# Modulation vectors of a two-layer decoder trunk: other phases, another pace, and VectorE for all

## Chip, core and metric

One core of a Trainium2 chip runs the whole kernel. The metric is the device time of one execution in microseconds. TensorE (PE in the profile, PEld for its weight loads), VectorE (DVE), ScalarE (ACT), GpSimd (POOL) and SyncE (SP, which issues nearly all DMAs) work at the same time and wait for one another by semaphores.

## The reference

Two layers over 256 tokens of width 1024. Each is a feed-forward block, a mixer of four parallel branches and another feed-forward block, and each of the three is modulated by three vectors (shift, scale, gate) that come from a conditioning vector `c`. There are nine such vectors of 1024 values per layer, each a product of `silu(c)` with a 1024x1024 slice of `ada_w`.

```python
D_MODEL, SEQ, DEPTH, D_FF, N_ADA = 1024, 256, 2, 2816, 9
def modulate(x, shift, scale): return x * (1.0 + scale) + shift
def swiglu(u, w1, w3, w2):     return (jax.nn.silu(u @ w1) * (u @ w3)) @ w2
# one layer, m = nine modulation vectors of c; s, b, g = shift, scale, gate of a phase
#   x = x + 0.5*(1+g1) * swiglu(modulate(rmsnorm(x), s1, b1))          first feed-forward
#   x = x + (1+g2) * W_out(sum_b sigmoid(G_b) * P_b(branch_b(u)))      mixer, u = modulate(rmsnorm(x), s2, b2)
#   x = x + 0.5*(1+g3) * swiglu(modulate(rmsnorm(x), s3, b3))          second feed-forward
# branches: RG-LRU (convolution + scan), latent attention, indexer-sparse attention, diagonal S5
```

## The kernel before

**Precision and tiling.** All weights lie in DRAM as float32. Each weight tile of 512 KB is loaded by a DMA of SyncE into a `raw` buffer (five of them), ScalarE rounds it into `hi` (`S.copy`, the CAST of L237), VectorE forms the rest `lo = raw - hi` (L103, L238), and TensorE does three matmuls for each product: hi·hi, hi·lo, lo·hi (`mm3`, `mm3w`, L243 to L251). The activations `uh`, `ul` are split in the same way (L371 for `uh`). So each weight tile costs one DMA, one ScalarE cast and one VectorE subtraction, and the split is emitted at a high priority.

**Phases.** Per layer: `ffn` (phase 0), `mixer` (phase 1), `ffn` (phase 2). The text calls them ffn1, mixer and ffn2. In the mixer an order written out by hand (`ORDER`, L66) calls the stages one after another: `za`, `zc`, `zb` are pieces of the input projection, `xr` the RG branch (convolution `r_conv`, matmuls L991 into `ps_acc_rg_states`), `us` and `S1` the S5 branch's input and states (L863, `ps_acc_s_states`; VectorE's `p_s_states`), `S2`, `GL`, `ix`, `m`, `da` the rest of the branches and the two attentions, `gnh` a half of gate n, `pnh` a half of branch projection n with its merge, `t0`, `t1` the merged halves, then `w_out` (`ps_acc_mixer`).

**Modulation vectors.** `ada(l, j)` (L265) is a generator that computes vector j of layer l in nine steps. Eight steps each load 512 KB of `ada_w` into a `raw` buffer (L274) and add its product with a column of `c`: on VectorE into `acc` (one `tensor_scalar`, L280, and seven `scalar_tensor_tensor`, recorded at L106), or, where `ADA_PE` names the vector, on TensorE into a PSUM bank (L277). A vector on VectorE is closed on TensorE by a sum over partitions with a matrix of ones (L287, eight matmuls in the profile). The ninth step's work adds the bias (`mrow`, L103/L294), and writes gates (j mod 3 = 2) to DRAM (L298, L300) or transposes shifts and scales on TensorE (L305, two matmuls) into a column (L307). Sixteen vectors are computed in this way; vectors 0 and 1 of layer 0 at the program's beginning are done otherwise.

**Pace.** `ADA` (L43) lists which vectors belong to which phase, as numbers j, where 9 and above are vectors of the next layer. `RATE` (L44) is the pace: each weight tile constructed (class `W`, L219) calls `tick()` (L210), which adds the phase's rate to a counter and runs one step of the generator for every whole number:

```python
    def tick():
        bg["n"] += bg["rate"]
        while bg["n"] >= 1.0:
            bg["n"] -= 1.0
            next(bg["gen"], None)
```

The stage `a` of `ORDER` runs whatever is left of the generator. Up to where `a` stands in the new order, a mixer constructs 70 weight tiles. Vectors 6 and 7 of a layer (shift and scale of its ffn2) are needed when the mixer's tail forms the next `uh` (`inputs_of`, L1489), vectors 3 and 4 when ffn1's tail does, vectors 2, 5 and 8 as gates in the tails of the three phases.

## Time and profile before

| | us |
|---|---|
| median of 3 runs | 1500.77 |
| lowest, highest run | 1494.9, 1513.13 |
| profiled execution | 1495.38 |
| span of its trace, first to last instruction | 1493.6 |
| TensorE busy | 1413.4 (95%) |
| VectorE busy | 1175.4 (79%) |
| ScalarE busy | 770.0 (52%) |
| mean granted clock of TensorE | 0.990 of full speed |

The phases of the span begin with the first u-matmul of each: the mixer of layer 0 at 245 us, its ffn2 at 580, ffn1 of layer 1 at 777, the mixer of layer 1 at 985, its ffn2 at 1301. Busy times of several engines lie over one another. A granted clock of 1.00 is 2.4 GHz, 0.50 is 1.2 GHz. A timeline entry with "x4" stands for four instructions of one kind in a row. The name behind "<-" in brackets is what ended the engine's idle time.

### The profile page before, as it was taken

Reading aid. Unit: us, or ns where it says so; the run is one execution under the profiler, and the core shown is the slowest. Engines: PE = TensorE matmul, PEld = TensorE weight load, DVE = VectorE, ACT = ScalarE, POOL = GpSimd, SP = SyncE. Lnnn points to the kernel's source line nnn. Section 1 sums busy time; section 2 is a strip of 40 time slices with the busy share of each in tenths; the row PEclk is TensorE's granted clock in tenths of the full one; section 3 lists DMA queues with packets and bytes.
Section 4 is the critical chain, followed back from the end, with each engine's and each line's share of the span. In section 5 each row is a group of like instructions: output and inputs, shape, how many; then the busy total and the mean of one; then the engine's idle time right before and its main releaser. Section 6 shows DMA issues by size and latency. Waiting matters only on the chain.

```text
span 1493.6 us, 26644 instructions
## 1 busy us (share of the span) xinstructions
PE 1413.4 (95%) x10310; PEld 1262.7 (85%) x10310; DVE 1175.4 (79%) x2027; ACT 770.0 (52%) x1223; POOL 64.0 (4%) x75
## 2 busy tenths in 40 slices
PE   8899999899998998999989998999999999999998
PEld 4588987789888897999968887879988879799997
DVE  4598988789897577988787888777998956866655
ACT  4444456654475645544453445568445655544442
POOL 0000000001011000000010000000100100000000
PEclk9999999999999999999999999999999999999999
DMA  9788888786435365899977878755653535567762
GB/s 287 236 288 291 280 260 258 228 222 174 114 117 138 99 187 181 286 328 317 320 252 250 271 254 276 246 135 143 174 146 95 140 94 164 162 214 227 235 203 99
DMA packets 242087, 313.24 MB, mean 210 GB/s; under 512 B 28088, under 2 KB 169256, under 8 KB 241960
## 3 DMA queue, kind: packets, MB, share of 16 engines
q1 hardware_dynamic: 241960, 311.53, 67.0%
q8 instruction: 81, 1.33, 0.4%
q14 instruction: 46, 0.38, 0.1%
HBM read 310.41 MB, written 1.07 MB: 209 GB/s over the span
## 4 chain that ended last, share of the span: by engine, by line
PE 55%; DVE 21%; DMA 11%; issue 6%; ACT 5%; POOL 1%; SPq 1%; POOLq 0%; DVEq 0%; ACTq 0%
DVE lo_genexpr L103 7%; DMA raw_ada<-in_ada_w_dram 5%; PE ps_up_up_half L249 5%; PE ps_up_up_half L250 5%; PE ps_up_up_half L251 5%; DMA raw_init<-in_ffn_w_dram 4%; PE ps_acc_down_proj L246 3%; PE ps_acc_down_proj L245 3%; PE ps_acc_down_proj L244 3%; PE ps_up_gate L250 3%; ACT hi_genexpr L237 3%; PE ps_up_gate L249 3%; PE ps_up_gate L251 3%; DVE acc_ada L106 2%; PE ps_up_merge L250 2%
## 5 line engine op out<-in xcount | busy, mean ns | idle before, releaser
L237 ACT CAST hi_genexpr<-raw_init 128x1024 fp32r<-128x1024 f32 (+2 forms) x430 | 441.1, 1028 | 497.2 <-PE ps_up_up_half L250 127.4
L103 DVE TENSOR_TENSOR lo_genexpr<-raw_init,hi_genexpr 128x1024 fp32r<-128x1024 f32 (+2 forms) x430 | 511.5, 1193 | 152.5 <-ACT hi_genexpr L237 150.1
L249 PE MATMUL ps_up_up_half<-uh_new_u,hi_genexpr 128*128 128x256 f32 x1216 | 339.2, 279 | 4.2 <-DVE p_silu_cols L106 1.6
L250 PE MATMUL ps_up_up_half<-ul_new_u,hi_genexpr 128*128 128x256 f32 x1216 | 337.4, 278 | 0.0
L251 PE MATMUL ps_up_up_half<-uh_new_u,lo_genexpr 128*128 128x256 f32 x1216 | 337.2, 278 | 0.1
L249 PEld LDWEIGHTS ps_up_up_half<-uh_new_u,hi_genexpr 128*128 128x128 f32 x1216 | 228.8, 188 | 9.8 <-issue 7.5
L250 PEld LDWEIGHTS ps_up_up_half<-ul_new_u,hi_genexpr 128*128 128x128 f32 x1216 | 228.7, 188 | 1.4
L251 PEld LDWEIGHTS ps_up_up_half<-uh_new_u,lo_genexpr 128*128 128x128 f32 x1216 | 228.2, 188 | 0.7 <-DVE lo_genexpr L103 0.7
L106 DVE SCALAR_TENSOR_TENSOR acc_ada<-raw_ada,c_col_tile_trunk,acc_ada 128x1024 f32<-128x1024 f32 x105 | 134.4, 1280 | 28.6 <-DMA raw_ada<-in_ada_w_dram 28.2
L250 PE MATMUL ps_up_gate<-ul_new_u,hi_genexpr 128*128 128x256 f32 x512 | 144.8, 283 | 0.0
L249 PE MATMUL ps_up_gate<-uh_new_u,hi_genexpr 128*128 128x256 f32 x512 | 144.6, 282 | 0.0
L251 PE MATMUL ps_up_gate<-uh_new_u,lo_genexpr 128*128 128x256 f32 x512 | 143.6, 280 | 0.0
L246 PE MATMUL ps_acc_down_proj<-hi_genexpr,yT_mul_cols 128*128 128x512 f32 x288 | 114.6, 398 | 0.0
L244 PE MATMUL ps_acc_down_proj<-hi_genexpr,yT_mul_cols 128*128 128x512 f32 x288 | 114.5, 397 | 0.0
L245 PE MATMUL ps_acc_down_proj<-lo_genexpr,yT_mul_cols 128*128 128x512 f32 x288 | 114.3, 397 | 0.1
L249 PEld LDWEIGHTS ps_up_gate<-uh_new_u,hi_genexpr 128*128 128x128 f32 x512 | 96.4, 188 | 3.0 <-issue 2.2
L251 PEld LDWEIGHTS ps_up_gate<-uh_new_u,lo_genexpr 128*128 128x128 f32 x512 | 96.7, 189 | 0.9 <-issue 0.8
L250 PEld LDWEIGHTS ps_up_gate<-ul_new_u,hi_genexpr 128*128 128x128 f32 x512 | 96.4, 188 | 1.1 <-issue 1.0
L244 PEld LDWEIGHTS ps_acc_down_proj<-hi_genexpr,yT_mul_cols 128*128 128x128 f32 x288 | 54.1, 188 | 13.1 <-issue 1.6
L245 PEld LDWEIGHTS ps_acc_down_proj<-lo_genexpr,yT_mul_cols 128*128 128x128 f32 x288 | 54.2, 188 | 12.6 <-DVE lo_genexpr L103 0.6
L246 PEld LDWEIGHTS ps_acc_down_proj<-hi_genexpr,yT_mul_cols 128*128 128x128 f32 x288 | 54.1, 188 | 12.3
L244 PE MATMUL ps_up_tok_gemm<-hi_genexpr,uh_new_u 128*128 128x424 f32 (+2 forms) x88 | 33.8, 385 | 2.7 <-ACT gt_gate L112 2.7
(474 smaller groups left out, 2698.1 us busy)
## 6 DMA issues: line engine op xcount, KB each, us to landing
raw_init<-in_ffn_w_dram SPq DMA_DIRECT2D x240, 512.0 KB
raw_ada<-in_ada_w_dram SPq DMA_DIRECT2D x128, 512.0 KB
raw_init<-in_w_in_dram SPq DMA_DIRECT2D x96, 512.0 KB
raw_init<-in_w_branch_dram SPq DMA_DIRECT2D x24, 512.0 KB
raw_init<-in_ffn_w_dram SPq DMA_DIRECT2D x36, 256.0 KB
raw_init<-in_w_out_dram SPq DMA_DIRECT2D x16, 512.0 KB
s5p_load<-in_ada_w_dram SPq DMA_DIRECT2D x16, 256.0 KB
s5p_load<-in_ada_w_dram SPq DMA_DIRECT2D x8, 512.0 KB
```

The lines of the kernel that those rows point to most:

```text
L103: eng.tensor_tensor(o, x, y, op)
L106: V.scalar_tensor_tensor(o, x, s, y, op0, op1)
L237: S.copy(self.hi, self.raw)
L244: T.matmul(o, xh, wh, start=first, stop=False)
L245: T.matmul(o, xh, wl, start=False, stop=False)
L246: T.matmul(o, xl, wh, start=False, stop=last)
L249: T.matmul(o, wh, xh, start=first, stop=False)
L250: T.matmul(o, wh, xl, start=False, stop=False)
L251: T.matmul(o, wl, xh, start=False, stop=last)
```

## The change

Four things. `ADA` gives two vectors (6 and 7) to the mixer of layer 1, which had none, and takes one each from ffn2 of layer 0 (five to four) and from ffn1 of layer 1 (four to three); sixteen vectors are computed as before. `RATE` lowers the pace of both mixers to 0.27 steps a weight tile (from 1.03 and 1.0), and of those two feed-forwards to 0.65 and 0.52. The TensorE variant of the product is gone: vector 7 of layer 0, the one that used it, goes to VectorE. And the stage `a` moves in `ORDER` from behind `gr S1` to behind `g21`, near the mixer's end.

```diff
-ADA = (((2, 3, 4, 5), (6, 7), (8, 9, 10, 11, 12)), ((4, 5, 6, 7), (), (8,)))
-RATE = ((0.67, 1.03, 0.81), (0.68, 1.0, 0.2))
+ADA = (((2, 3, 4, 5), (6, 7), (8, 9, 10, 11)), ((3, 4, 5), (6, 7), (8,)))
+RATE = ((0.67, 0.27, 0.65), (0.52, 0.27, 0.2))
-ADA_PE = ((7, 10, 9, 11), ())
-ORDER = """za xr xr us xr S1 xr g01 S1 gr S1 a zc S1 g00 S1 ix S2 g30 p01 S2 g20 S2 ix ix p00 ix m S2 S2 m m g31 zb m GL da p30 ix m m p31 da g10 da m m g11 p20 p10 g21 p11 p21 t0 t1"""
+ORDER = """za xr xr us xr S1 xr g01 S1 gr S1 zc S1 g00 S1 ix S2 g30 p01 S2 g20 S2 ix ix p00 ix m S2 S2 m m g31 zb m GL da p30 ix m m p31 da g10 da m m g11 p20 p10 g21 a p11 p21 t0 t1"""
     def ada(l, j):
-        on_pe = j in ADA_PE[l % 2]
-        if on_pe:
-            p = bank("ms")
-        else:
-            acc = new("acc", (128, 1024))
+        acc = new("acc", (128, 1024))
         for k in range(KD):
...
-            if on_pe:
-                for q in range(4):
-                    T.matmul(p[32 * q:32 * q + 32, 0:256], bc(c_col[:, k:k + 1], (128, 32)), raw[:, 256 * q:256 * q + 256],
-                             start=(k == 0), stop=(k == KD - 1), tile_position=(0, 32 * q))
-            elif k == 0:
+            if k == 0:
                 V.tensor_scalar(acc, raw, c_col[:, k:k + 1], None, OP.mult)
...
-        if not on_pe:
-            p = bank("ms")
-            for q in range(4):
-                T.matmul(p[32 * q:32 * q + 32, 0:256], ones, acc[:, 256 * q:256 * q + 256], start=True, stop=True,
-                         tile_position=(0, 32 * q))
+        p = bank("ms")
+        for q in range(4):
+            T.matmul(p[32 * q:32 * q + 32, 0:256], ones, acc[:, 256 * q:256 * q + 256], start=True, stop=True,
+                     tile_position=(0, 32 * q))
```

Lines of the new kernel stand about ten lower: L106 becomes L105, L103 becomes L102, L287 becomes L277, L305 becomes L295.

VectorE in the mixer of layer 0, at the convolution of the RG branch (`r_conv` rows), before: two steps of vector 6 (`acc_ada`) stand in twelve rows. Each row is line, operation, output<-inputs, shape.

```order
L103 TENSOR_TENSOR mll_mla_in_2757<-ps_tp_ev_2840,mlh_mla_in_2756 128x3x128
L106 SCALAR_TENSOR_TENSOR r_conv_2885<-r_conv_2882,vt_params_699,r_conv_2885 128x256
L975 MEMSET r_conv_2924 128x3
L106 SCALAR_TENSOR_TENSOR acc_ada_2853<-raw_ada_3050,c_col_tile_trunk_86,acc_ada_2853 128x1024
L103 TENSOR_TENSOR lo_genexpr_3117<-raw_init_3114,hi_genexpr_3116 128x1024
L106 SCALAR_TENSOR_TENSOR r_conv_2885<-r_conv_2882,vt_params_699,r_conv_2885 128x256
L106 SCALAR_TENSOR_TENSOR r_conv_2927<-r_conv_2924,vt_params_699,r_conv_2927 128x256
L975 MEMSET r_conv_2966 128x3
L106 SCALAR_TENSOR_TENSOR acc_ada_2853<-raw_ada_3085,c_col_tile_trunk_86,acc_ada_2853 128x1024
L103 TENSOR_TENSOR lo_genexpr_3152<-raw_init_3149,hi_genexpr_3151 128x1024
L106 SCALAR_TENSOR_TENSOR r_conv_2927<-r_conv_2924,vt_params_699,r_conv_2927 128x256
L106 SCALAR_TENSOR_TENSOR r_conv_2969<-r_conv_2966,vt_params_699,r_conv_2969 128x256
```

The same place now:

```order
L105 SCALAR_TENSOR_TENSOR r_conv_2881<-r_conv_2878,vt_params_699,r_conv_2881 128x256
L965 MEMSET r_conv_2917 128x3
L105 SCALAR_TENSOR_TENSOR r_conv_2881<-r_conv_2878,vt_params_699,r_conv_2881 128x256
L105 SCALAR_TENSOR_TENSOR acc_ada_2970<-raw_ada_3137,c_col_tile_trunk_86,acc_ada_2970 128x1024
L102 TENSOR_TENSOR lo_genexpr_3070<-raw_init_3067,hi_genexpr_3069 128x1024
L105 SCALAR_TENSOR_TENSOR r_conv_2881<-r_conv_2878,vt_params_699,r_conv_2881 128x256
L105 SCALAR_TENSOR_TENSOR r_conv_2920<-r_conv_2917,vt_params_699,r_conv_2920 128x256
L965 MEMSET r_conv_2956 128x3
L105 SCALAR_TENSOR_TENSOR r_conv_2920<-r_conv_2917,vt_params_699,r_conv_2920 128x256
L102 TENSOR_TENSOR lo_genexpr_3102<-raw_init_3099,hi_genexpr_3101 128x1024
L105 SCALAR_TENSOR_TENSOR r_conv_2920<-r_conv_2917,vt_params_699,r_conv_2920 128x256
L105 SCALAR_TENSOR_TENSOR r_conv_2959<-r_conv_2956,vt_params_699,r_conv_2959 128x256
```

One step is left among these rows. The numbers count the buffers in the order in which they are taken, so this step, on `raw_ada_3137`, stands ahead of the subtraction `lo` 3070 of a weight tile whose load was issued before. Over the whole convolution, five steps stood among the rows and one does now.

TensorE in the mixer of layer 0, in a gate (`ps_up_gate`), before: one of the eight places at which vector 7 is multiplied.

```order
L250 MATMUL ps_up_gate_3237<-ul_new_u_2577,hi_genexpr_3287 128x256
L251 MATMUL ps_up_gate_3237<-uh_new_u_2576,lo_genexpr_3288 128x256
L249 MATMUL ps_up_gate_3237<-uh_new_u_2576,hi_genexpr_3287 128x256
L250 MATMUL ps_up_gate_3237<-ul_new_u_2577,hi_genexpr_3287 128x256
L251 MATMUL ps_up_gate_3237<-uh_new_u_2576,lo_genexpr_3288 128x256
L277 MATMUL ps_ms_ada_3291<-raw_ada_3330,c_col_tile_trunk_86 32x256 x4
```

Now there is no such place; what a vector has on TensorE is its closing sum and, eight rows later, its two transposes, here those of vector 6 in `g20`:

```order
L248 MATMUL ps_up_gate_4145<-uh_new_u_2576,hi_genexpr_4148 128x256
L249 MATMUL ps_up_gate_4145<-ul_new_u_2577,hi_genexpr_4148 128x256
L250 MATMUL ps_up_gate_4145<-uh_new_u_2576,lo_genexpr_4149 128x256
L277 MATMUL ps_ms_ada_4182<-acc_ada_2970,ones_tile_trunk_98 32x256 x4
L248 MATMUL ps_up_gate_4145<-uh_new_u_2576,hi_genexpr_4178 128x256
L249 MATMUL ps_up_gate_4145<-ul_new_u_2577,hi_genexpr_4178 128x256
L250 MATMUL ps_up_gate_4145<-uh_new_u_2576,lo_genexpr_4179 128x256
L248 MATMUL ps_up_gate_4145<-uh_new_u_2576,hi_genexpr_4178 128x256
L249 MATMUL ps_up_gate_4145<-ul_new_u_2577,hi_genexpr_4178 128x256
L250 MATMUL ps_up_gate_4145<-uh_new_u_2576,lo_genexpr_4179 128x256
L248 MATMUL ps_up_gate_4145<-uh_new_u_2576,hi_genexpr_4178 128x256
L295 MATMUL ps_tp_ada_4194<-cst_tile_trunk_75,mrow_ada_4192 128x128 x2
```

The eight groups of `L277 x4` are gone; the closing sum and the transposes of a vector stand within one gate, with matmuls of that gate between them.

VectorE in the mixer of layer 1, at the S5 states (`p_s_states`), before:

```order
L103 TENSOR_TENSOR lo_genexpr_12091<-raw_init_12088,hi_genexpr_12090 128x1024
L103 TENSOR_TENSOR b_s_states_11586<-p_s_states_11763,p_s_states_11764 128x4x63
L103 TENSOR_TENSOR b_s_states_11586<-p_s_states_11764,p_s_states_11763 128x4x63
L103 TENSOR_TENSOR p_s_states_11869<-p_s_states_11869,p_s_states_11870 128x256 x2
L103 TENSOR_TENSOR s_rope_12030<-dc_dsa_in_11777,cosT_tile_trunk_101 128x64
L874 SCALAR_TENSOR_TENSOR p_s_states_11870<-s5p_s_prep_9965,p_s_states_11869 128x256
L103 TENSOR_TENSOR lo_genexpr_12121<-raw_init_12118,hi_genexpr_12120 128x1024
L874 SCALAR_TENSOR_TENSOR p_s_states_11870<-s5p_s_prep_9965,p_s_states_11869 128x256
L103 TENSOR_TENSOR s_rope_12031<-dc_dsa_in_11777,sinT_tile_trunk_100 128x64
L103 TENSOR_TENSOR p_s_states_11869<-p_s_states_11870,s5p_s_prep_10118 128x512
L103 TENSOR_TENSOR s_rope_12032<-dc_dsa_in_11777,cosT_tile_trunk_101 128x64
```

The same place now:

```order
L102 TENSOR_TENSOR lo_genexpr_12007<-raw_init_12004,hi_genexpr_12006 128x1024
L102 TENSOR_TENSOR p_s_states_11674<-p_s_states_11674,s5p_s_prep_10041 128x512
L102 TENSOR_TENSOR p_s_states_11782<-p_s_states_11782,p_s_states_11783 128x256
L102 TENSOR_TENSOR b_s_states_11493<-p_s_states_11673,p_s_states_11674 128x4x63
L102 TENSOR_TENSOR b_s_states_11493<-p_s_states_11674,p_s_states_11673 128x4x63
L102 TENSOR_TENSOR lo_genexpr_12037<-raw_init_12034,hi_genexpr_12036 128x1024
L102 TENSOR_TENSOR p_s_states_11782<-p_s_states_11782,p_s_states_11783 128x256
L105 SCALAR_TENSOR_TENSOR acc_ada_11100<-raw_ada_11866,c_col_tile_trunk_86,acc_ada_11100 128x1024
L102 TENSOR_TENSOR lo_genexpr_12072<-raw_init_12069,hi_genexpr_12071 128x1024
L864 SCALAR_TENSOR_TENSOR p_s_states_11783<-s5p_s_prep_9874,p_s_states_11782 128x256 x2
L869 MEMSET b_s_states_11790 128x8
L102 TENSOR_TENSOR s_rope_11946<-dc_dsa_in_11687,cosT_tile_trunk_101 128x64
```

A step of vector 6 of layer 1 (`acc_ada_11100`) has come between two weight tiles' subtractions.

## Rows read from the trace of the kernel before

**Rows 1.** The page's first part: busy time, share of the span, instructions.

```profile
PE 1413.4 (95%) x10310; PEld 1262.7 (85%) x10310; DVE 1175.4 (79%) x2027; ACT 770.0 (52%) x1223; POOL 64.0 (4%) x75
```

**Rows 2.** Table by stretch: start:end, us, busy us (count) PE PEld DVE ACT POOL, clock, DMA share, GB/s.

```profile
245.00:580.00 335.00, 313.16 (x2435) 285.23 (x2436) 270.32 (x544) 187.49 (x356) 22.65 (x22) 0.98 0.57 162
580.00:777.00 197.00, 190.79 (x1340) 171.76 (x1339) 167.76 (x249) 94.27 (x122) 1.55 (x2) 1.00 0.87 297
...
985.00:1301.00 316.00, 299.41 (x2358) 276.47 (x2358) 259.47 (x527) 186.77 (x356) 20.77 (x20) 1.00 0.50 142
```

**Rows 3.** Timeline of PE where the phases begin: start, us, instruction, [idle before <-releaser].

```profile
245.09 0.72 PE L244 MATMUL ps_up_tok_gemm<-dq_genexpr,uh_new_u 128*128 128x416 f32 x1 [2.17 <-ACT uh_new_u L371]
...
579.68 0.50 PE L244 MATMUL ps_up_up_proj<-s5p_genexpr,uh_new_u 128*128 128x512 f32 x1 [2.78 <-ACT uh_new_u L371]
...
776.80 0.79 PE L244 MATMUL ps_up_up_proj<-s5p_genexpr,uh_new_u 128*128 128x512 f32 x1 [2.77 <-ACT uh_new_u L371]
...
985.28 0.46 PE L244 MATMUL ps_up_tok_gemm<-dq_genexpr,uh_new_u 128*128 128x416 f32 x1 [1.00 <-ACT uh_new_u L371]
...
986.86 0.45 PE L246 MATMUL ps_up_tok_gemm<-dq_genexpr,ul_new_u 128*128 128x416 f32 x1 [0.93 <-DVE ul_new_u L103]
...
1301.07 0.50 PE L244 MATMUL ps_up_up_proj<-s5p_genexpr,uh_new_u 128*128 128x512 f32 x1 [1.01 <-ACT uh_new_u L371]
```

**Rows 4.** Tile ps_acc_s_states, window of either mixer: ns min/median/max, first to last start.

```profile
L863 PE MATMUL ps_acc_s_states<-b_s_states,s5p_s_prep x64: 217/275/275, 309.7 to 351.9; 128*128 128x64 f32 x64
...
L863 PE MATMUL ps_acc_s_states<-b_s_states,s5p_s_prep x64: 217/275/323, 1036.0 to 1076.0; 128*128 128x64 f32 x64
```

**Rows 5.** Table by stretch, short windows in the two mixers, columns as in group 2.

```profile
245.00:265.00 20.00, 19.91 (x117) 19.13 (x117) 17.00 (x29) 12.77 (x34) 3.04 (x3) 0.85 0.78 223
265.00:285.00 20.00, 15.42 (x98) 14.29 (x97) 15.75 (x27) 10.55 (x21) 0.06 (x1) 0.83 0.83 240
...
1060.00:1076.00 16.00, 16.00 (x135) 15.97 (x134) 16.00 (x33) 8.06 (x15) 0.00 (x0) 1.00 0.68 187
```

**Rows 6.** Timeline of PE in the mixer of layer 0, columns as in group 3.

```profile
271.90 0.89 PE L991 MATMUL ps_acc_rg_states<-r_conv,rgw_tile_trunk 128*128 128x256 f32 x3 [1.18 <-issue]
...
275.87 1.62 PE L991 MATMUL ps_acc_rg_states<-r_conv,rgw_tile_trunk 128*128 128x256 f32 x3 [2.87 <-DVE r_conv L106]
...
299.79 0.44 PE L305 MATMUL ps_tp_ada<-cst_tile_trunk,mrow_ada 128*128 128x128 f32 x2 [2.63 <-DVE mrow_ada L103]
300.15 0.64 PE L277 MATMUL ps_ms_ada<-raw_ada,c_col_tile_trunk 128*32 128x256 f32 x8
```

**Rows 7.** Timeline of DVE in the mixer of layer 0, columns as in group 3.

```profile
272.12 1.28 DVE L106 SCALAR_TENSOR_TENSOR acc_ada<-raw_ada,c_col_tile_trunk,acc_ada 128x1024 f32<-128x1024 f32 x1
...
274.45 1.67 DVE L106 SCALAR_TENSOR_TENSOR r_conv<-r_conv,vt_params,r_conv 128x256 f32<-128x256 f32 x4
```

**Rows 8.** Tile raw_ada, whole span: operations, and who waited for the tile (us, times).

```profile
L106 DVE SCALAR_TENSOR_TENSOR acc_ada<-raw_ada,c_col_tile_trunk,acc_ada x105: 1262/1279/1289, 77.1 to 1412.1; 128x1024 f32<-128x1024 f32 x105
...
L277 PE MATMUL ps_ms_ada<-raw_ada,c_col_tile_trunk x64: 379/390/403, 300.2 to 327.7; 128*32 128x256 f32 x64
L280 DVE TENSOR_SCALAR acc_ada<-raw_ada,c_col_tile_trunk x15: 739/746/2939, 71.5 to 1311.2; 128x1024 f32<-128x1024 f32 x15
...
  DVE acc_ada L106: 28.2, 33
```

**Rows 9.** Tiles acc_ada and mrow_ada, whole span, columns as in group 8.

```profile
L287 PE MATMUL ps_ms_ada<-acc_ada,ones_tile_trunk x120: 379/391/403, 112.5 to 1438.7; 128*32 128x256 f32 x120
...
  PE ps_tp_ada L305: 5.7, 4
```

**Rows 10.** Tile ps_acc_down_proj, the second feed-forwards of layers 0 and 1, columns as in group 4.

```profile
L246 PE MATMUL ps_acc_down_proj<-hi_genexpr,yT_mul_cols x76: 390/399/402, 635.0 to 773.6; 128*128 128x512 f32 x76
...
L246 PE MATMUL ps_acc_down_proj<-hi_genexpr,yT_mul_cols x76: 390/399/403, 1356.2 to 1488.7; 128*128 128x512 f32 x76
```

**Rows 11.** Waits of DVE in 245 to 580: who <- releaser: us, times, longest.

```profile
DVE acc_ada L280 <- DMA raw_ada<-in_ada_w_dram: 0.6, 1, 0.6
```

## The prediction

> **What bounds the kernel now.** The first look is at the busy times of the whole span: TensorE has work in 1413.4 of 1493.6 us [rows 1], so at most 80 us of waiting is there to win, plus what a lower clock costs. The second is the table by phase [rows 2]: the mixer of layer 0 leaves TensorE idle for 335.0 − 313.2 = 21.8 us at a mean granted clock of 0.98, the second feed-forward of layer 0 moves 297 GB/s at a DMA share of 0.87, and the mixer of layer 1, which has no modulation vector, leaves VectorE idle for 316.0 − 259.5 = 56.5 us, at clock 1.00.
>
> The third look compares the two mixers, which do the same work apart from two vectors. Each begins with its first u-matmul, at 245.09 and 985.28 [rows 3]. The last state matmul of the S5 branch starts at 351.9 and 1076.0 [rows 4], so 106.8 and 90.7 us later: layer 0 is 16.1 us behind after a third of its mixer. Over the whole phase, to the next feed-forward's first matmul (579.68 and 1301.07), it is 334.6 against 315.8, or 18.8 longer. Of these, 1.8 is the longer wait at the end (2.78 against 1.01, [rows 3]), so 17.0 belong to the mixer and nearly all of them arise in the stretch where both vectors stand.
>
> What happens there, in two 20 us windows and the timelines: the clock granted is 0.85 and 0.83 of full speed [rows 5], that is (0.15 + 0.17) × 20 = 6.4 us of full-speed work lost; TensorE waits 1.18, 2.87 and 2.63 us (together 6.7) [rows 6], the second for a row of the RG convolution on VectorE, the third for a vector's result row. VectorE at that moment alternates `r_conv` rows with `acc_ada` steps of 1.28 us; [rows 7] shows one of each, right before the 2.87 us wait ends. Vector 7, on TensorE, has eight groups of eight matmuls of 0.64 us a group [rows 6], 64 in all [rows 8], 5.1 us. That makes 18.2 against the 17.0 of the comparison, which is close since layer 1 has small waits of its own.
>
> **The change part by part.** The sum starts from the profiled execution, 1495.4 us (span 1493.6); the median of the runs shown, 1500.8, lies 5.4 above it.
>
> 1. *The vectors of mixer 0 leave the first 80 us.* The rate of 1.03 becomes 0.27 steps a weight tile, so vector 6, with nine steps, ends near the 9 / 0.27 = 34th of 70 tiles and vector 7 near the 67th, and one step instead of five stands among the convolution rows. Vector 7 costs TensorE no 64 matmuls. So the 17.0 us should come back, but part of the clock loss in the first window follows the phase change: the granted clock was low right behind the 2.17 us wait at 245.09. That window lost 0.15 × 20 = 3.0 us; I leave half, 1.5, in place. Gain: −15.5. At the two ends it is −17.0, or nothing if the waits only move to other rows.
>
> 2. *What two spread vectors cost a mixer; call it c.* No row of before shows a vector strung over a mixer. Each has on VectorE 0.746 + 7 × 1.279 = 9.70 us [rows 8], 19.4 for two, in a phase with 56.5 us of VectorE idle in layer 1. TensorE must still issue the closing sum (eight matmuls, as 120 for 15 vectors [rows 9]; by the group of eight in rows 6 0.64 us) and two transposes, 0.44 [rows 6]: 2.2 us for two vectors. It waits for the result row 5.7 us in all [rows 9] in ten transposing vectors (16 less the six gates, by the code), 0.57 each, 1.1 for two. And the steps find VectorE full in the S5 stretch (16.00 of 16 us [rows 5]), where a step of 1.28 pushes a `lo` that TensorE needs: one such per vector, 2.6. So c = 2.2 + 1.1 + 2.6 = 5.9. Bounds: 2.2, since TensorE's own share can't hide while it is the bound (that also excludes a gain in layer 1, where nothing is removed); and 19.4 + 2.2 = 21.6 if every step lies on the path. I take 5.9, nearer to the low end, because 56.5 us of idle is three times the load.
>  Mixer 0: +5.9. Mixer 1, which had none: +5.9.
>
> 3. *One vector fewer in ffn2 of layer 0 (5 to 4) and in ffn1 of layer 1 (4 to 3).* The price per vector is read from ffn2: with five vectors 579.68 to 773.6 = 193.9 us, with one 1301.07 to 1488.7 = 187.6 [rows 3, 10]; 6.3 for four, 1.6 each. Bounds: 0.64, the closing sum alone, and 10.3, all its VectorE time and that sum. I take 1.6, the one direct comparison, for both: −3.2. The eight loads of 512 KB each move along with the vector, from phases with a DMA share of 0.87 to one with 0.50 [rows 2].
>
> 4. *The change from ffn2 to layer 1.* TensorE waits 2.77 us there, for ScalarE's `uh`, where the crossing into mixer 1 has 1.00 + 0.93 and that into the last phase begins with 1.01 [rows 3]. In the new order no `hi` cast stands between ScalarE's last tail piece and the `uh` casts. I take 2.77 − 1.93, −0.8 (ends: 0 and −2.8).
>
> 5. *The drain `a` at the end of the mixer* is at no cost: by then at most the last of 18 steps is left, and what it hides behind is the gate matmuls of `g21`. If steps remained, each would cost 1.28.
>
> Sum: −15.5 + 5.9 + 5.9 − 3.2 − 0.8 = −7.7, so 1495.4 − 7.7 = **1487.7 us**.
>
> One rule speaks against step 2. In rows 8 the `acc_ada` steps had VectorE waiting for their load 33 times, 28.2 us in all, or 0.27 us for each of 105 steps. The Trainium skill, in "TensorE: Matmul & The Clock Gate", section "Architectural detail: the array is 16× 32×32, not 1× 128×128", says that only TensorE's queue may pull weight loads ahead, and that VectorE and ScalarE work strictly first in, first out; so a step whose load is late holds every `lo` behind it. By the row's 0.27 us a step that is 16 × 0.27 = 4.3 us a mixer at most, and the sum would be 1487.7 + 2 × 4.3 = 1496.3; where it also starves TensorE, it is the third rival.
>
> **The rivals.** A change of 2%, 30 us, is about what a measurement of this kernel can tell from none.
>
> *Nothing is gained.* The 15.5 come back but the vectors cost as much again: c of (15.5 + 3.2 + 0.8) / 2 = 9.8, half of the VectorE time. For it: VectorE is full for tens of us in the S5 stretch, where the new order now has steps. Against: 56.5 us of idle. About 1495.
>
> *Larger gain.* Spread steps all fit into idle time, c = 2.2, and the whole 17.0 comes back: 1495.4 − 17.0 + 4.4 − 4.0 = 1478.8, with the 4.0 of the parts 3 and 4. For it: feed-forward hides a vector at 1.6, which is below my 2.9. Against: the transposes wait in every phase.
>
> *Slower.* VectorE takes its instructions in order, and in the new order `acc_ada` steps stand ahead of `lo` rows whose weights were loaded before (`raw_ada` 3137 ahead of `lo` 3070). A weight step then waits for a vector's load, and the vector's load holds one of five `raw` buffers until VectorE comes to it, which in the full stretch is dozens of rows later. If each mixer then pays what mixer 0 paid, 17.0: 1495.4 − 15.5 + 34.0 − 4.0 = 1509.9. It decides from c over 9.8. For it: the 28.2 us of such waits over the whole program [rows 8]. Against: in mixer 0, with two vectors, VectorE waited so only once, 0.6 us [rows 11]; the mixers move 162 and 142 GB/s, the feed-forward 297 [rows 2].
>
> **How the numbers follow.** Forecast 0.50, nothing gained 0.20, larger gain 0.16, slower 0.14. The range takes in the gain of 1478.8 with a spread of 5 below it, and the slower end 1509.9: 1474 to 1510. For the forecast itself, c from 2.2 to 9.0 gives 1480 to 1494. All four lie within 30 us of the present time; for over 2% the feed-forward prices would have to be near 10 each and c low (0.03 faster), or c near 21.6 in both mixers, 1495.4 − 15.5 + 43.2 − 4.0 = 1519, with more waits on top (0.03 slower).
>
> **What would show it.** Right: mixer 0 reaches the last state matmul about 93 us after its start (106.8 now), the clock in its second window is 1.00, the 2.87 us wait for `r_conv` is gone, and mixer 1's same distance grows by under 4. Whole mixers: near 325 and 322 us, from 334.6 and 315.8. The `ffn` phases lose 1 to 3 us. Wrong: mixer 1 longer by over 10 us, or VectorE waits for `raw_ada` in the mixers in place of `hi`, or mixer 0 keeps its low clock behind the phase change, which would mean that the vectors were not its cause.

## The result and the profile after

The new kernel takes 1521.45 us (median of 4 runs, 1518.46 to 1524.97) against 1500.88 of the kernel before (4 runs beside it): a ratio of 1.0141, with a 95% interval of 1.0103 to 1.0178. It is slower by 1.4%, where 1487.7 was forecast and 1510 was the upper end of the range. Its profiled execution took 1520.93 us, 25.6 more than that of before. Ratios, here and below, leave out the executions that took over 1.5% more than the fastest of their kernel, among them one of `b_both_pe` with 1745 us at a granted clock of 0.75; the medians keep them.

The table by stretch, cut at the phases of the new kernel (start:end, us, busy us and count of PE PEld DVE ACT POOL, clock, DMA share, GB/s), answers to [rows 2]:

```profile
0.00:243.80 243.80, 224.26 (x1515) 181.52 (x1515) 193.03 (x365) 118.14 (x172) 10.81 (x21) 0.99 0.86 277
243.80:581.83 338.03, 313.52 (x2379) 288.04 (x2379) 278.29 (x550) 187.33 (x354) 23.27 (x22) 0.96 0.56 161
581.83:780.34 198.51, 193.79 (x1329) 175.03 (x1330) 154.60 (x235) 96.22 (x123) 1.10 (x2) 0.97 0.81 271
780.34:990.70 210.36, 199.42 (x1365) 178.99 (x1364) 161.71 (x215) 99.78 (x128) 8.62 (x10) 0.98 0.72 224
990.70:1326.48 335.78, 311.71 (x2378) 285.78 (x2378) 278.12 (x547) 186.81 (x355) 22.81 (x20) 0.97 0.55 159
1326.48:1519.10 192.62, 185.86 (x1292) 169.42 (x1292) 118.06 (x128) 82.81 (x96) 1.47 (x1) 1.00 0.62 192
```

Against before (phase starts from [rows 3]): the start is 1.3 us shorter, the mixer of layer 0 is 338.0 instead of 334.6, ffn2 198.5 instead of 197.1, ffn1 of layer 1 210.4 instead of 208.5, the mixer of layer 1 **335.8 instead of 315.8**, the last phase the same. These are −1.3 + 3.4 + 1.4 + 1.9 + 20.0 + 0.1 = 25.5 us. Nothing came back in layer 0's mixer, nothing in the feed-forwards that lost a vector each, and the mixer that received two vectors pays 20 us. Note VectorE's column there: 335.8 − 278.1 leaves 57.7 us idle, and before it was 56.5. The added work, 278.1 − 259.3 = 18.8 us, did not go into the idle time; the phase grew by as much.

The timeline of PE at the phase starts of the new kernel (the rows of [rows 3] in their new form), and its two S5 state rows (tile ps_acc_s_states, [rows 4]):

```profile
581.83 0.51 PE L243 MATMUL ps_up_up_proj<-s5p_genexpr,uh_new_u 128*128 128x512 f32 x1 [2.77 <-ACT uh_new_u L361]
...
990.70 0.46 PE L243 MATMUL ps_up_tok_gemm<-dq_genexpr,uh_new_u 128*128 128x416 f32 x1 [1.02 <-ACT uh_new_u L361]
...
992.27 0.72 PE L245 MATMUL ps_up_tok_gemm<-dq_genexpr,ul_new_u 128*128 128x416 f32 x1 [0.92 <-DVE ul_new_u L102]
```

```profile
L853 PE MATMUL ps_acc_s_states<-b_s_states,s5p_s_prep x64: 217/275/323, 294.3 to 337.6; 128*128 128x64 f32 x64
...
L853 PE MATMUL ps_acc_s_states<-b_s_states,s5p_s_prep x64: 217/275/421, 1042.9 to 1088.2; 128*128 128x64 f32 x64
```

In layer 0 the last state matmul now starts 337.6 − 243.8 = 93.8 us into the mixer, as forecast (93, from 106.8). So the early stretch did get its time back, and the rest of that mixer gave it away again. In layer 1 it is 1088.2 − 990.7 = 97.5, 6.8 more than the 90.7 of before, where less than 4 was forecast.

The waits of PE in the new mixer of layer 1 (who <- releaser: total us, times, longest), the first of them:

```profile
PE ps_acc_s_out_prep L807 <- DVE s5p_s_out_prep L105: 3.4, 1, 3.4
PE ps_acc_s_states L853 <- DVE r_gate L105: 3.0, 1, 3.0
PE ps_tp_attend L1121 <- DVE p_attend L102: 2.6, 1, 2.6
PE ps_tp_mla L1339 <- DVE s5p_mla L102: 2.3, 1, 2.3
```

In the kernel before, the longest row of this mixer and the one for `r_gate` are:

```profile
PE ps_tp_mla L1349 <- DVE s5p_mla L103: 2.5, 2, 1.5
PE ps_acc_s_states L863 <- DVE r_gate L106: 0.9, 1, 0.9
```

All four of the new kernel end with a short VectorE operation of a branch: `s5p_s_out_prep`, `r_gate`, `p_attend`, `s5p_mla`. In the new kernel's layer 0 the same four stand, with nearly the same lengths, before the matmuls at 360.65, 310.75, 451.95 and 427.42 us. What VectorE did before the longest of them is seen in its timeline; PE waited from 1107.80 to 1111.22:

```profile
1106.16 1.29 DVE L102 TENSOR_TENSOR p_s_out_prep<-s5Cc_s_prep,s5pw_s_prep 128x512 f32<-128x512 f32 x2
1107.36 1.28 DVE L105 SCALAR_TENSOR_TENSOR acc_ada<-raw_ada,c_col_tile_trunk,acc_ada 128x1024 f32<-128x1024 f32 x1
1108.56 1.22 DVE L102 TENSOR_TENSOR lo_genexpr<-raw_init,hi_genexpr 128x1024 fp32r<-128x1024 f32 x1
1109.69 1.38 DVE L105 SCALAR_TENSOR_TENSOR s5p_s_out_prep<-p_s_out_prep,p_s_out_prep 64x512 f32<-64x512 f32 x2
```

The operation that TensorE needs runs at 1109.69. In the 2.3 us ahead of it stand a vector's step (1.28 us) and a weight's `lo`. VectorE does not pause in these rows, so what stands behind an added step starts later by the step's length.

The order in which TensorE's matmuls run has changed as well. The 64 matmuls of the tile `ps_acc_s_out_prep` in the mixer of layer 1, before and now:

```profile
L817 PE MATMUL ps_acc_s_out_prep<-s5p_s_out_prep,s5bd_s_prep x64: 272/273/297, 1105.7 to 1107.5; 128*32 128x128 f32 x64
...
L807 PE MATMUL ps_acc_s_out_prep<-s5p_s_out_prep,s5bd_s_prep x64: 269/273/322, 1106.7 to 1127.3; 128*32 128x128 f32 x64
```

Before, they stand together behind a gate's matmuls and start within 1.8 us. Now sixteen of them stand ahead of a gate's matmuls, the second eight being the ones that wait 3.4 us, and the other 48 behind it. So a part of this wait may come from the place that the matmuls have in this order, and not from VectorE alone.

The granted clock behind two of these waits, in 5 us windows of the new kernel:

```profile
1055.00:1060.00 5.00, 1.98 (x17) 1.70 (x15) 5.00 (x12) 1.49 (x4) 0.00 (x0) 1.00 1.03 256
1060.00:1065.00 5.00, 5.00 (x21) 4.81 (x21) 4.41 (x11) 1.40 (x4) 1.90 (x2) 0.53 0.68 199
1065.00:1070.00 5.00, 5.00 (x23) 4.78 (x22) 2.23 (x4) 2.91 (x5) 0.00 (x0) 0.79 0.04 8
...
1110.00:1115.00 5.00, 3.54 (x23) 3.28 (x24) 4.96 (x8) 0.00 (x0) 0.00 (x0) 0.66 0.58 160
```

TensorE has 1.98 of 5 us of work in the window of the wait, and in the next two the clock is 0.53 and 0.79 of full speed; after the other wait it is 0.66. That is (0.47 + 0.21) × 5 = 3.4 and 0.34 × 5 = 1.7 us of full-speed work, on top of the waits themselves. Over the phase the clock is 0.97 where before had 1.00 [rows 2].

### The profile page after: what moved, and what is told of

Its sections match the earlier page's. It is cut to its first block, busy times and chain, and to the rows that moved or that the text cites. A ratio compares the mean times of both kernels' runs of the same rounds, so it can differ in the third digit from the quotient of the medians.

```text
span 1519.1 us, 26553 instructions
## 1 busy us (share of the span) xinstructions
PE 1428.6 (94%) x10254; PEld 1278.8 (84%) x10254; DVE 1183.8 (78%) x2035; ACT 771.1 (51%) x1223; POOL 68.1 (4%) x75
## 4 chain that ended last, share of the span: by engine, by line
PE 64%; DVE 18%; DMA 7%; ACT 4%; issue 4%; POOL 2%; SPq 0%; POOLq 0%; DVEq 0%; ACTq 0%
PE ps_up_up_half L248 6%; PE ps_up_up_half L249 6%; PE ps_up_up_half L250 6%; DVE lo_genexpr L102 6%; DMA raw_ada<-in_ada_w_dram 5%; PE ps_acc_down_proj L245 4%; PE ps_acc_down_proj L244 3%; PE ps_acc_down_proj L243 3%; PE ps_up_gate L248 3%; PE ps_up_gate L249 3%; PE ps_up_gate L250 3%; DMA raw_init<-in_ffn_w_dram 2%; ACT hi_genexpr L236 2%; DVE acc_ada L105 2%; PE ps_up_merge L248 2%
## 5 line engine op out<-in xcount | busy, mean ns | idle before, releaser
L102 DVE TENSOR_TENSOR lo_genexpr<-raw_init,hi_genexpr 128x1024 fp32r<-128x1024 f32 (+2 forms) x430 | 511.1, 1194 | 137.6 <-ACT hi_genexpr L236 134.3
L105 DVE SCALAR_TENSOR_TENSOR acc_ada<-raw_ada,c_col_tile_trunk,acc_ada 128x1024 f32<-128x1024 f32 x112 | 143.5, 1281 | 55.2 <-DMA raw_ada<-in_ada_w_dram 55.1
L248 PE MATMUL ps_up_gate<-uh_new_u,hi_genexpr 128*128 128x256 f32 x512 | 148.7, 290 | 3.2 <-DVE p_merge L105 2.0
```

The costliest lines, as they stand in the source:

```text
L102: eng.tensor_tensor(o, x, y, op)
L105: V.scalar_tensor_tensor(o, x, s, y, op0, op1)
L248: T.matmul(o, wh, xh, start=first, stop=False)
```

## The experiments

Theory A, after this look: the steps' multiplications on VectorE (28 of 1.28 us, fourteen in each mixer) delay short operations that TensorE waits for; neither the loads nor the vectors' part on TensorE matters. All lengths of phases below are read from the same table by stretch, cut at each kernel's own phase starts, of one profiled execution each. The mixer of layer 1 without vectors came out between 315.8 and 321.7 us in seven kernels, so a difference of under 6 us in one mixer can't be told from chance.

| | median us | ratio to before (95%) | mixer layer 0 | mixer layer 1 |
|---|---|---|---|---|
| before | 1500.88 | | 334.6 | 315.8 (no vectors) |
| new | 1521.45 | 1.0141 (1.0103 to 1.0178) | 338.0 | 335.8 |
| a_mix1_empty | 1506.70 | 1.0062 (1.0039 to 1.0085) | 338.9 | 320.8 (none) |
| a_no_products | 1490.53 | 0.9947 (0.9917 to 0.9977) | 324.1 | 322.5 |
| a_no_loads | 1521.40 | 1.0165 (1.0146 to 1.0185) | 338.0 | 335.4 |
| a_half | 1526.29 | 1.0153 (1.0086 to 1.0220) | 339.9 | 340.0 |
| a_late | 1513.20 | 1.0077 (1.0043 to 1.0110) | 333.5 | 330.8 |
| a_pool | 1563.55 | 1.0404 (1.0348 to 1.0460) | 356.2 | 362.9 |
| a_pe | 1506.82 | 1.0037 (1.0001 to 1.0074) | 330.3 | 332.3 |
| b_both_pe | 1495.08 | 0.9966 (0.9936 to 0.9995) | 326.7 | 321.7 (none) |
| b_late | 1497.43 | 0.9987 (0.9963 to 1.0011) | 333.2 | 316.4 (none) |
| b_mix0_empty | 1522.89 | 1.0127 (1.0078 to 1.0176) | 319.5 (none) | 321.0 (none) |
| c_567_pe | 1499.48 | 0.9992 (0.9954 to 1.0029) | 337.4 (three) | 316.1 (none) |
| c_5pe_ffn | 1502.57 | 1.0016 (0.9975 to 1.0057) | 328.2 | 316.1 (none) |

**Which part of the change: the vectors of layer 1's mixer.**

```diff
-ADA = (((2, 3, 4, 5), (6, 7), (8, 9, 10, 11)), ((3, 4, 5), (6, 7), (8,)))
-RATE = ((0.67, 0.27, 0.65), (0.52, 0.27, 0.2))
+ADA = (((2, 3, 4, 5), (6, 7), (8, 9, 10, 11, 12)), ((4, 5, 6, 7), (), (8,)))
+RATE = ((0.67, 0.27, 0.81), (0.68, 0.27, 0.2))
```

> The new kernel with the vector lists of before (mixer of layer 1 empty, five vectors in ffn2 of layer 0, four in ffn1 of layer 1, paces 0.81 and 0.68); the mixer pace of 0.27, the late drain and all vectors on VectorE stay. Theory A (two spread vectors cost a mixer about 20 us, a vector in a feed-forward costs next to nothing): mixer of layer 1 falls from 335.8 to about 316, total about 1501, the time of the kernel before. Rival (the new order of instructions as a whole costs the time, whatever vectors it carries): mixer of layer 1 stays above 330, total above 1515.

Measured: 1506.7 us, the mixer of layer 1 at 320.8, each 5 to 6 us above what theory A gave and far from the rival's figures. The two vectors of that mixer are 15 us of the loss. The profile is of the longest of the four executions (1512.6), 17.1 us longer than that of before: 4.3 in layer 0's mixer (338.9), 5.0 in this empty mixer, which has a clock of 0.98 where that of before had 1.00, and 7.7 in the start and in ffn1 of layer 1, which carry the same vectors as before:

```profile
997.21:1317.97 320.76, 304.54 (x2358) 281.41 (x2359) 259.49 (x526) 186.26 (x355) 20.76 (x20) 0.98 0.48 140
```

**Which part of a vector: the multiplications, the loads, or the closing on TensorE.** In `a_no_products` the seven accumulating steps of vectors 6 and 7 are left out, so their result is the first eighth of each sum:

```diff
-            else:
+            elif j not in (6, 7):
                 stt(acc, raw, c_col[:, k:k + 1], acc, OP.mult, OP.add)
```

> The new kernel; of vectors 6 and 7 of both layers (the mixers' four) the seven scalar_tensor_tensor steps are left out, their loads, the first step, the closing sum and the transposes stay. Theory A (the steps of 1.28 us stand on VectorE ahead of short operations of the branches that TensorE waits for): both mixers fall from 338 and 336 to about 318, the waits of 3.0 us for r_gate and 3.4 us for s5p_s_out_prep go, clock near 0.99, total about 1485. Rival B (the loads and the raw buffers they hold): no change, 1515 to 1525. Rival C (closing sum and transposes on TensorE): no change either.

In `a_no_loads` seven of eight loads are left out, and the steps work on the accumulator:

```diff
-            raw = new("raw", (128, 1024))
-            nc.sync.dma_start(raw, a["ada_w"][l, k * 128:(k + 1) * 128, j * D:(j + 1) * D])
+            if k == 0 or j not in (6, 7):
+                raw = new("raw", (128, 1024))
+                nc.sync.dma_start(raw, a["ada_w"][l, k * 128:(k + 1) * 128, j * D:(j + 1) * D])
...
-                stt(acc, raw, c_col[:, k:k + 1], acc, OP.mult, OP.add)
+                stt(acc, acc if j in (6, 7) else raw, c_col[:, k:k + 1], acc, OP.mult, OP.add)
```

> The new kernel; of the mixers' four vectors seven of eight loads are left out, and the seven steps multiply the accumulator itself instead of the loaded tile (same shape and operation). Theory A: the steps are still on VectorE, so mixers stay near 336 and the total at 1510 to 1525. Rival B (loads, raw buffers): mixers fall to about 318, total about 1485. Half and half would be 1500.

Measured: without the multiplications 1490.5, some 5 us above what theory A gave, and without the loads 1521.4, where the new kernel has 1521.5. The rows of the two mixers, first of `a_no_products`, then of `a_no_loads`:

```profile
244.83:568.89 324.06, 305.38 (x2379) 281.78 (x2379) 262.50 (x536) 186.42 (x354) 21.37 (x22) 0.98 0.57 168
974.89:1297.41 322.52, 305.45 (x2379) 281.42 (x2379) 261.58 (x533) 186.38 (x355) 20.75 (x20) 0.99 0.56 166
```

```profile
243.06:581.06 338.00, 316.52 (x2378) 292.18 (x2379) 279.50 (x550) 187.24 (x354) 23.19 (x22) 0.95 0.48 139
991.45:1326.84 335.39, 313.95 (x2379) 289.02 (x2379) 278.49 (x547) 186.98 (x355) 23.56 (x20) 0.96 0.48 138
```

The 28 multiplications are 28 × 1.28 = 35.8 us of VectorE, and the two mixers are shorter by 13.97 + 13.26 = 27.2 us without them, three quarters of their duration. Of the 27.2, TensorE's idle time (us less PE's busy time in the rows) makes 5.8 + 7.0 = 12.8. The other 14.4 are busy time of TensorE, for the same number of matmuls at a clock of 0.96 and 0.97 instead of 0.98 and 0.99. So in these executions about half of the price of the steps is waiting and about half is the lower clock. The 3.0 us wait for `r_gate` is 0.9 in layer 1 there, the one for `s5p_s_out_prep` is gone, and the 64 matmuls of `ps_acc_s_out_prep` start within 1.8 us again. That the steps are the cause is shown; how much they cost as delay on VectorE and how much through the changed order of the instructions is not separated by these runs.

All loads, the first step, the closing sum and the transposes stay in `a_no_products`. Together they are 324.1 − 319.5 = 4.6 us in layer 0 and 322.5 − 318.3 = 4.2 in layer 1, against the empty mixer of layer 0 (`b_mix0_empty`) and the mean of the seven of layer 1; the prediction gave the closing and its waits 3.3. Differences of this size are within what an empty mixer varies.

`a_no_loads` shows that the price is there without the loads (139 GB/s in layer 0's mixer, 161 in the new kernel) and without `raw` buffers held by a vector, which the third rival of the prediction was built on. It is no proof that they cost nothing, because the steps stand elsewhere in it. The steps in the mixer of layer 1, of the new kernel and then of `a_no_loads` (first to last start):

```profile
L105 DVE SCALAR_TENSOR_TENSOR acc_ada<-raw_ada,c_col_tile_trunk,acc_ada x14: 1256/1280/1286, 1011.7 to 1237.2; 128x1024 f32<-128x1024 f32 x14
...
L105 DVE SCALAR_TENSOR_TENSOR acc_ada<-acc_ada,c_col_tile_trunk x14: 1267/1279/1286, 1002.0 to 1129.8; 128x1024 f32<-128x1024 f32 x14
```

Without loads the seven steps of each vector follow one another within 25 us, and TensorE's longest waits are others: 2.1 us for `r_conv` and 2.9 for `s5p_mla`, with `r_gate` at 0.9. Two placements of the same work came to the same time.

**Is it the length of one step.** `a_half` cuts each step of the mixers' vectors into two.

```diff
-                stt(acc, raw, c_col[:, k:k + 1], acc, OP.mult, OP.add)
+                for h in range(2 if j in (6, 7) else 1):
+                    x = slice(512 * h, 512 * h + 512) if j in (6, 7) else slice(0, 1024)
+                    stt(acc[:, x], raw[:, x], c_col[:, k:k + 1], acc[:, x], OP.mult, OP.add)
```

> The new kernel with each of the seven accumulating steps of the mixers' four vectors cut into two halves of 512 columns, which stand apart in VectorE's order. If one long step in the way of a short operation is the price, halves are shorter to wait for: mixers fall by 4 to 8 us each, total 1505 to 1513. If the price is VectorE's time itself in stretches where TensorE and VectorE hand work to and fro (each step late by its own length wherever it stands), halves cost as much or a little more: total 1519 to 1528.

Measured: 1526.3, mixers 339.9 and 340.0; a half step took 744 ns, so the two together 0.21 us more than one. Shorter pieces bring nothing: the total is in the range of the second case, a price that goes with VectorE's time and not with the length of one step.

**Does the place decide.** `a_late` and `b_late` begin the vectors late, from the stage `GL` on; their first steps start 173 to 174 us into the mixer.

```diff
-RATE = ((0.67, 0.27, 0.65), (0.52, 0.27, 0.2))
+RATE = ((0.67, 0.0, 0.65), (0.52, 0.0, 0.2))
+        stages["b"] = once(lambda: bg.update(rate=0.95))
```

In `ORDER` the new stage `b` stands between `GL` and `da`.

> The new kernel with the mixers' vectors begun only at the 50th weight tile of the mixer (pace 0 before, 0.95 from the stage GL on), where VectorE is busy for 11 to 15 of 20 us in the trace of before; same vectors, same drain. Theory A (what counts is whether VectorE has idle time where the steps stand): both mixers fall from 338 and 336 to 322 to 327, total 1493 to 1503. Rival D (a step costs about 1 us of TensorE wherever it stands in a mixer): mixers stay at 335 to 338, total 1515 to 1525.

For `b_late` the same on the kernel before, with both vectors on VectorE and the drain `a` behind `g21`:

```diff
-RATE = ((0.67, 1.03, 0.81), (0.68, 1.0, 0.2))
+RATE = ((0.67, 0.0, 0.81), (0.68, 0.0, 0.2))
-ADA_PE = ((7, 10, 9, 11), ())
+ADA_PE = ((), ())
+        stages["b"] = once(lambda: bg.update(rate=0.95))
```

> The kernel before with its two vectors of the mixer of layer 0 both on VectorE and begun late in the same way, drain behind g21; lists otherwise as before. Theory A: mixer 0 falls from 334.6 to 322 to 327, the rest stays, total 1486 to 1492, under the kernel before. Rival D: mixer 0 stays at 335 to 338, total within 4 us of before.

Measured: 333.5 and 330.8 in `a_late`, 333.2 in `b_late`: 4.5 to 5 us better per mixer than the new kernel, about as much as an empty mixer varies, and between what the two theories gave. In total `a_late` took 1513.2 us, also between them, and `b_late` 1497.4, which is within 4 us of before, the case of rival D. The waits of PE in the mixer of layer 1 of `a_late` show what remains:

```profile
PE ps_tp_attend L1121 <- DVE p_attend L102: 5.9, 4, 2.5
PE ps_ms_attend L1126 <- ACT p_attend L115: 3.0, 5, 0.7
```

The S5 waits are gone (`r_gate` back to 0.9), and the attention waits instead, 5.9 us for `p_attend` in four waits, where the kernel before has one of 0.9. VectorE's share of idle time in a window did not say here that work fits there: in the attention TensorE waits for VectorE's tiles (these rows), and a step put among them can make them late.

**On another engine.** `a_pool` gives the steps to GpSimd as two operations each, `a_pe` all mixer vectors to TensorE, `b_both_pe` layer 0's second one in the kernel before.

```diff
-                stt(acc, raw, c_col[:, k:k + 1], acc, OP.mult, OP.add)
+                if j in (6, 7):
+                    G.tensor_scalar(raw, raw, c_col[:, k:k + 1], None, OP.mult)
+                    G.tensor_tensor(acc, acc, raw, OP.add)
+                else:
+                    stt(acc, raw, c_col[:, k:k + 1], acc, OP.mult, OP.add)
```

> The new kernel; the seven accumulating steps of each of the mixers' four vectors go to GpSimd as a multiplication and an addition, which has work in 4% of the span. Theory A (they block VectorE's queue): VectorE's rows for r_gate and s5p_s_out_prep come in time and mixers fall to 322 to 330. Rival E (GpSimd's operations are long or slow VectorE's down when both run, and the norm steps that GpSimd does wait behind them): mixers at 340 or more, total above 1525.

Measured: 1563.6 us, mixers of 356.2 and 362.9, the rival's case (above 1525, mixers at 340 or more). The groups of GpSimd and then of VectorE in the mixer of layer 1 of `a_pool`, and two of VectorE's in the new kernel's (count | busy us, mean ns | idle before):

```profile
L274 POOL TENSOR_SCALAR raw_ada<-raw_ada,c_col_tile_trunk 128x1024 f32<-128x1024 f32 x14 | 46.9, 3350 | 116.2 <-DMA raw_ada<-in_ada_w_dram 56.9 <-ACT p_dsa_index L111 25.9 <-DVE m_dsa_index L1205 10.9
L275 POOL TENSOR_TENSOR acc_ada<-acc_ada,raw_ada 128x1024 f32<-128x1024 f32 x14 | 35.7, 2553 | 1.1
...
L102 DVE TENSOR_TENSOR s5p_merge<-s5p_merge,p_merge 128x512 f32<-128x512 f32 x12 | 10.6, 887 | 0.1
...
L102 DVE TENSOR_TENSOR p_s_states<-p_s_states,s5p_s_prep 128x512 f32<-128x512 f32 x8 | 7.6, 954 | 0.0
```

```profile
L102 DVE TENSOR_TENSOR s5p_merge<-s5p_merge,p_merge 128x512 f32<-128x512 f32 x12 | 8.2, 687 | 0.1
...
L102 DVE TENSOR_TENSOR p_s_states<-p_s_states,s5p_s_prep 128x512 f32<-128x512 f32 x8 | 5.5, 687 | 0.0
```

A step takes 3.35 + 2.55 us on GpSimd, and VectorE's own operations grow while it runs: 687 to 887 ns and 687 to 954. VectorE lost 14 steps of 1.28 us in this mixer and is still busier, 296.5 us against 278.1.

For `a_pe` the kernel before is edited, which still has the code for TensorE:

```diff
-ADA = (((2, 3, 4, 5), (6, 7), (8, 9, 10, 11, 12)), ((4, 5, 6, 7), (), (8,)))
-RATE = ((0.67, 1.03, 0.81), (0.68, 1.0, 0.2))
+ADA = (((2, 3, 4, 5), (6, 7), (8, 9, 10, 11)), ((3, 4, 5), (6, 7), (8,)))
+RATE = ((0.67, 1.03, 0.65), (0.52, 1.03, 0.2))
-ADA_PE = ((7, 10, 9, 11), ())
+ADA_PE = ((6, 7), (6, 7))
```

> The new lists of vectors (two in each mixer, four in ffn2 of layer 0, three in ffn1 of layer 1), but both vectors of each mixer on TensorE, at the old pace and with the old place of the drain. Theory A (VectorE's products are the price, not where the vectors belong): mixer of layer 0 near 327, of layer 1 near 322 to 327, feed-forwards unchanged, total 1493 to 1502. Rival (a second mixer with vectors costs 15 to 20 us in any form): total above 1510.

Measured: 1506.8, 5 us above what theory A gave; layer 0 at 330.3 (expected 327), layer 1 at 332.3 (expected up to 327). VectorE's time is not the whole price of a vector: on TensorE its 64 matmuls take 5.1 us (eight groups of 0.64, as in [rows 6]), twice that is 10.2, and the measured price is 332.3 − 318.3 = 14.0 in layer 1, against the mean of the seven empty ones (315.8, 320.8, 321.7, 316.4, 321.0, 316.1, 316.1), and 330.3 − 319.5 = 10.8 in layer 0. It is still 14.6 us less in all than on VectorE, though the pace and the place of the drain differ too.

```diff
-ADA_PE = ((7, 10, 9, 11), ())
+ADA_PE = ((6, 7, 10, 9, 11), ())
```

> The kernel before with vector 6 of layer 0 on TensorE as vector 7 is, nothing else changed. Theory A: the 2.87 us wait for r_conv and the low clock behind it go (about 3 us and 3.4 us), eight groups of 0.64 us come (+5.1, less 0.6 for the closing sum): total within 5 us of the kernel before. If the products on VectorE had cost mixer 0 nothing: 4.5 us slower.

Measured: 1495.1 us, a ratio of 0.9966 (0.9936 to 0.9995): mixer 0 at 326.7, 7.9 less than before. Its row shows the clock at 0.99 where before had 0.98 [rows 2]:

```profile
243.62:570.28 326.66, 311.24 (x2490) 280.75 (x2491) 261.88 (x534) 187.13 (x354) 21.30 (x22) 0.99 0.56 166
```

It is the one version computing everything that came out faster than both kernels, by a third of a percent against before, with an interval that only just leaves out 1; one such interval among twelve edits can be chance.

**Other phases.** Can the vectors leave mixer 0 altogether?

```diff
-ADA = (((2, 3, 4, 5), (6, 7), (8, 9, 10, 11, 12)), ((4, 5, 6, 7), (), (8,)))
-RATE = ((0.67, 1.03, 0.81), (0.68, 1.0, 0.2))
-ADA_PE = ((7, 10, 9, 11), ())
+ADA = (((2, 3, 4, 5, 6, 7), (), (8, 9, 10, 11, 12)), ((4, 5, 6, 7), (), (8,)))
+RATE = ((1.0, 1.03, 0.81), (0.68, 1.0, 0.2))
+ADA_PE = ((), ())
```

> The kernel before with both vectors of mixer 0 moved to ffn1 of layer 0 (six there at a pace of 1.0, on VectorE), mixers empty. Theory A: mixer 0 falls to 316 to 322; ffn1 of layer 0 has VectorE busy for 17 to 20 of 20 us from 80 to 200 us, so it must pay for them, 8 to 15 us (ends at 252 to 259 from 245): total within 5 us of before. Rival (a vector in a feed-forward costs nothing, as the two phases of the result seem to say): start phase stays at 245, total about 1485.

Measured: mixer 0 fell to 319.5 as expected, but the start phase grew from 245.1 to 280.0, more than either theory gave. The next two kernels asked whether VectorE bounds that phase. `c_567_pe` moves vector 5 from ffn1 to mixer 0 and has all three there on TensorE; in `c_5pe_ffn` only the last line of this edit is made:

```diff
-ADA = (((2, 3, 4, 5), (6, 7), (8, 9, 10, 11, 12)), ((4, 5, 6, 7), (), (8,)))
-RATE = ((0.67, 1.03, 0.81), (0.68, 1.0, 0.2))
+ADA = (((2, 3, 4), (5, 6, 7), (8, 9, 10, 11, 12)), ((4, 5, 6, 7), (), (8,)))
+RATE = ((0.51, 1.55, 0.81), (0.68, 1.0, 0.2))
-ADA_PE = ((7, 10, 9, 11), ())
+ADA_PE = ((5, 6, 7), ())
```

> The kernel before with vector 5 of layer 0 moved from ffn1 to the mixer, and vectors 5, 6 and 7 there all on TensorE (paces 0.51 and 1.55). Six vectors made ffn1 of layer 0 35 us longer than four, so three should make it shorter, if VectorE bounds it below four too: start phase 230 to 238 instead of 245, mixer 0 329 to 331; total 1483 to 1492. If that phase is bound by TensorE at four vectors: start phase 243 to 245, total 1497 to 1500.

> The kernel before with vectors 5, 6 and 7 of layer 0 on TensorE where they are (5 in ffn1, 6 and 7 in the mixer). If VectorE bounds ffn1 of layer 0: start phase 236 to 241, mixer 0 near 327, total 1485 to 1493. If TensorE does: start phase 248 to 250, total 1497 to 1501.

Measured: start phases of 240.0 and 248.8, mixers of 337.4 and 328.2, totals equal to before. VectorE is not the bound of that phase: with one vector's VectorE work less and the same loads it was 3.7 us longer (248.8), what the expectation gave for TensorE as the bound. The start phase in the three kernels:

```profile
0.00:280.01 280.01, 243.39 (x1534) 192.02 (x1534) 213.03 (x386) 118.53 (x172) 12.53 (x21) 0.93 0.83 272
```

```profile
0.00:240.02 240.02, 222.91 (x1507) 181.68 (x1507) 183.26 (x353) 117.12 (x170) 10.86 (x20) 0.98 0.81 263
```

```profile
0.00:248.81 248.81, 231.48 (x1571) 184.76 (x1571) 183.36 (x354) 116.93 (x170) 10.60 (x20) 0.98 0.84 271
```

TensorE as the bound fits only one of the three: 240.0 is below the 243 of that case, and two vectors more on VectorE add only their closings to TensorE's work. Loads fit no better. The DMA share is 0.81 to 0.84 and the rate 263 to 272 GB/s; sixteen loads of 512 KB more are 8.4 MB, 31 us at 272 GB/s, of the 35 that were added, but eight fewer should give 16 and gave 5, and the 3.7 us came with no load more. Of the 35 us, 18 are idle time of TensorE (36.6 here, 18.7 before) and 17 its busy time, at a clock of 0.93 where before had 0.98. What bounds ffn1 of layer 0 stays open.

## Why the prediction was wrong

**What bounds, and step 1** (the vectors of mixer 0 leave the early stretch): right. It gave the early stretch back, though the mixer as a whole did not get shorter. The distance to the last state matmul was forecast at 93 us and is 93.8; the 2.87 us wait for `r_conv` and the 2.63 for `mrow_ada` are gone; the window from 260 to 280 us has a clock of 1.00. The two vectors of before were worth 334.6 − 319.5 = 15.1 us by `b_mix0_empty`, one execution against one, and the step had 15.5.

**Step 2, the price c of two spread vectors: here the prediction failed.** The term was sized at 5.9 us a mixer. It measured 338.0 − 319.5 = 18.5 in layer 0 and 335.8 − 318.3 = 17.5 in layer 1 (15.0 against the one empty mixer of the same edit, `a_mix1_empty`), inside the bounds of 2.2 and 21.6 but near the end that was not taken. The part for VectorE, 2.6, stood for one step per vector that pushes a `lo`; measured are 13.97 and 13.26 us for fourteen (`a_no_products`). The wrong step in the reasoning was "56.5 us of idle is three times the load". The steps did not go into that idle time: it was 57.7 us with the vectors in and 322.5 − 261.6 = 60.9 without their multiplications. What ends it could have been read beforehand; the largest wait of VectorE in the mixer of layer 1, before and then now, and the largest of ScalarE before:

```profile
DVE lo_genexpr L103 <- ACT hi_genexpr L237: 24.0, 26, 2.5
```

```profile
DVE lo_genexpr L102 <- ACT hi_genexpr L236: 23.4, 21, 3.2
```

```profile
ACT hi_genexpr L237 <- PE ps_up_gate L250: 30.5, 20, 3.6
```

VectorE stands for 24.0 and 23.4 us at a `lo` whose `hi` is not there yet, ScalarE's `hi` waits for TensorE in turn, and TensorE waits for VectorE at the four rows above. So much of the idle time lies where VectorE is ahead of TensorE, and the steps stand elsewhere, as between two short operations that TensorE needs. That this is why the idle time was of no use is argued from these rows and was not tested by itself. The term also left out the clock: two waits of 3 us cost 6.4 us by themselves and 5.1 us of full-speed work in the windows behind them, and of the 27.2 us of the multiplications about half is slower matmuls.

**Step 3, one vector fewer in two feed-forwards:** −3.2 forecast, nothing measured. Over the 14 kernels, ffn2 of layer 0 takes 198.9 us on average with five vectors (seven kernels, 197.1 to 201.7) and 198.6 with four (seven, 197.1 to 199.9); ffn1 of layer 1 takes 209.6 with four and 209.2 with three. The 1.6 us per vector came from comparing the ffn2 of the two layers, which differ in more than their vectors.

**Step 4, the crossing into layer 1:** nothing. The wait at the first matmul is gone, but one of 2.64 us stands ahead of it at 775.81 (for `b_tail`, 0.44 before) and one of 2.10 behind it at 783.11 (for `ul_new_u`).

**Step 5, the late drain:** no cost was seen; the last closing sum of mixer 1 starts by 1278.5, 48 us ahead of the phase's end.

**The rule on queues.** The rule of the Trainium skill ("TensorE: Matmul & The Clock Gate", section "Architectural detail: the array is 16× 32×32, not 1× 128×128") is that VectorE works strictly first in, first out. The timeline above agrees with it: 2.3 us of other work run ahead of `s5p_s_out_prep`. The term of 0.27 us per step for a late load was near in size, but it was not the price: in mixer 1 VectorE waited for `raw_ada` 3.1 us in all (tile raw_ada), of at most 4.3 by that term, and with seven of eight loads left out the mixer was as long.

**The rivals.** "Slower" came closest, 1509.9 against 1521, with 17.0 a mixer against 18.5 and 17.5; its 17.0 was taken over from mixer 0 of before, and that it came near is luck, since its mechanism of late loads and held buffers is not needed for the price (`a_no_loads`). With the measured terms its sum would be 1495.4 − 15.1 + 18.5 + 17.5 = 1516.3, and the missing 4.6 to the profiled 1520.9 lie in the feed-forwards (+3.3 there and −1.3 at the start) and in layer 1's mixer of before, at 315.8 below the mean of 318.3. The chance of 0.14 for it was too low by the profile's own rows: [rows 5] showed VectorE full for 16 of 16 us at the place where steps were put.

## What to carry to other kernels

Before background work goes to an engine because its share of idle time is large, look at what ends that idle time: in these mixers, where engines hand tiles to and fro, added work lengthened the phase by most of its duration (0.76 us per us), and the later place that was tried took off 4.5 to 5 us of some 18. The test is cheap: take out the work but leave its loads and its closing, then take out only the loads, and look each time whether the rest still runs in the same order. And a price per item has to come from two runs that differ in that item; two phases that look alike gave 1.6 us for something that costs nothing.
